# One long piece of projections per attention step, and value products between the two heads' transpositions

## The chip, the cores and the metric

The kernel runs on one NeuronCore of a Trainium2 chip. The metric is the device time of one execution in microseconds (us); the median of the runs shown is compared. TensorE is called PE here, VectorE DVE, ScalarE ACT, GpSimd POOL and the queue that issues most loads SP.

## The reference

A two-layer network over 256 latent and 256 context tokens (512 in all, width 1024). Each layer has four attention-like mixers that run side by side on one input projection, then an output projection, then a product-key expert network:

```python
(na_q, na_k, na_v, ml_qk, ml_v, ml_o, ml_g,
 mla_cq, mla_ckv, mla_kr, sw_q, sw_k, sw_v) = split_cols(h @ w_in)
...
y_a = neighbourhood_attention(...)      # 4 heads of 64
h_lat, h_ctx = mlstm_mixer(...)         # 4 heads
y_c = block_dense_attention(...)        # latent attention (MLA), keys from ckv and a shared rope part
y_d = window_attention(...)             # 4 query heads, 2 key heads, a sink
x = x + g1 * (jnp.concatenate([y_a, y_b, y_c, y_d], axis=-1) @ w_out)
...
f = peer_ffn(...)                       # top-16 of 128x128 experts for each of 8 heads
```

Layer 0 computes all 512 tokens in the mixers, layer 1 only the queries of the 256 latent ones. All data are 32-bit floats; projections are made of three products of a split operand (high and low parts).

## The kernel before

A layer is `mixers(l)` and then `peer(l)`. The expert part takes most of the time: layer 0's mixers run up to about 420 us of the span, its experts to about 1765 us, layer 1's mixers to about 1975 us, its experts to the end. The change lies in the mixers, in `run_units`.

**Units.** Each mixer makes units, one for each head and each block of 128 queries (`pairs`). A unit has 256 keys (query blocks 0 and 1, the context) or 512 keys (blocks 2 and 3). Units are worked off in pairs, the two heads of one query block. A mixer has 8 pairs in layer 0, two for each size twice over, and 4 pairs in layer 1, all of 512 keys. The order of the mixers is mLSTM (ML), neighbourhood (NA), latent attention (MLA), window (SW). For a pair PE makes the scores (`sc`), DVE and ACT make a softmax or the mLSTM's weights in SBUF (`soft`: for a softmax L582 the maximum, L588 the exponential with its sum, L592 and L593 the division), PE transposes each unit's weights into one PSUM bank (`tp`, L634; the pool `pst` has one buffer), ACT copies that to SBUF (L636), and PE multiplies by the values into `py` (L649). The scores of a pair are made one turn ahead, the value products one turn behind.

**The filler.** Projections that later mixers need are cut into small steps by generators. A `Filler` holds them in a queue, and `F.step(us)` issues steps until the sum of what they yield (an assumed time) reaches `us`, or until one yields 0:

```python
while us > 0:
    t = self._next()
    if t is None:
        return
    us -= t if t else us
```

So a step that yields 0 ends the whole call. The generators put such zeros where PE would wait for another engine: `mla_prep` (the normalisation, the rope and the small products of MLA) has 18 of them, two at the start and six before the scale of each of its two normalisations, one before each rope; `sw_prep` has one and `ada_end` four, at the end of layer 0's jobs for the modulation. Other steps are one k-block of a projection: three matmuls (L72, L73, L74), assumed at 0.65 us for 512 columns and 0.33 us for 256; for the modulation (L266, L267) two matmuls at 0.22 us. Before a mixer's first scores `F.finish(need)` issues without pause all that is left of the jobs which that mixer needs.

**A turn before.** The assumed time of one piece is `u.fill`: 1.3 us for ML in layer 0 and 2.0 in layer 1, 1.0 and 1.2 for NA, 1.2 and 1.2 for MLA, 1.2 and 1.0 for SW. A turn on a pair is: transpose the first unit; a piece; transpose the second unit; the next pair's scores; a piece; the last pair's value products; two pieces.

**What sets the order.** In the mixers PE's instructions stand as the program writes them (`manual_schedule`). The other engines, and PE in the expert part, are ordered by a scheduler that goes by its own estimate of times, so a change here can also move instructions elsewhere.

Of the kernel before, what the change touches and what calls it, by code (L numbers as in the profile page):

```python
# [8 lines left out]
F32 = mybir.dt.float32  # L9
# [44 lines left out]
class Kernel:  # L54
# [541 lines left out]
    def run_units(self, units):  # L596

        nc, F = self.nc, self.F  # L600
        n = len(units)
        p = {}
        py = None

        def score(i):
            if i >= n:
                return
            for u in units[i:i + 2 + AHEAD]:
                if u.pre:
                    F.finish(u.need)  # L610
                    u.pre()
                    u.pre = None
            both = units[i:i + 2]
            for u in both:
                F.finish(u.need)
            sc = [self.psc.tile([128, 512], F32, name="sc") for _ in both]
            steps = [u.score(x) for u, x in zip(both, sc)]
            while steps:
                steps = [g for g in steps if next(g, 0) is None]
            for j, u in enumerate(both):  # L620
                p[i + j] = u.soft(sc[j])
        score(0)
        F.step(1.0)
        F.step(1.0)
        last = None
        for i in range(0, n + 2, 2):
            both = units[i:i + 2]
            pts = []
            for j, u in enumerate(both):
                tp = self.pst.tile([128, 512], F32, name="tp")  # L630
                w = p.pop(i + j)
                nb = len(u.blocks)
                for x, kb in enumerate(u.blocks):
                    nc.tensor.transpose(tp[:, x * 128:(x + 1) * 128], w[:, kb * 128:(kb + 1) * 128], self.ident)  # L634
                pt = self.new()
                nc.scalar.copy(pt[:, :nb * 128], tp[:, :nb * 128])  # L636
                pts.append(pt)
                if j:
                    score(i + 2)
                F.step(u.fill)  # L640
            if last is not None:
                vs, vts = last
                if vs[0].first:
                    py = self.psy.tile([128, 512], F32, name="py")
                for x in range(max(len(v.blocks) for v in vs)):
                    for v, vt in zip(vs, vts):
                        nb = len(v.blocks)
                        if x < nb:
                            nc.tensor.matmul(py[v.rows, v.qt * 128:(v.qt + 1) * 128], v.v(v.blocks[x]), vt[:, x * 128:(x + 1) * 128],  # L649
                                             start=(x == 0), stop=(x == nb - 1))  # L650
                if vs[1].done:
                    vs[1].done(py)
                for v in vs:
                    F.step(v.fill)
            last = both, pts

    def put_y(self, ft, py, mul=None):
# [1145 lines left out]
```

## Time and profile before

| | us |
|---|---|
| median of the runs | 2815.85 |
| the profiled execution, its time | 2815.21 |
| its span | 2813.4 |
| PE busy in the span | 2649.8 |
| DVE busy | 2166.6 |
| ACT busy | 1244.3 |

The span is what the trace covers; its times count from the span's start. A wait that the timeline names in brackets is idle time of that engine just ahead of the row, with the instruction that ended it. Busy time of PE is modelled from starts and sizes, so the difference between two starts is the better price of a row. The granted clock is a mean over a stretch: 1.00 is 2.4 GHz all along, 0.50 would be 1.2 GHz all along.

### The profile page before, as it was taken

The page shows a single profiled execution, that of the slowest core. Times are in us where ns is not written, and L with a number is a line of the kernel's source. Part 1 is how long each engine was busy: PE and PEld are TensorE (multiplying, and loading weights), DVE is VectorE, ACT ScalarE, POOL GpSimd, SP SyncE. Part 2 cuts the span into 40 slices and gives each one's busy share as a digit, 9 for nine tenths or more (in the row PEclk, how much of TensorE's full clock was granted, in tenths as well). Part 3 has the DMA queues.
Part 4 walks back from the last instruction along what each step waited for, and adds up shares of the span by engine and source line. Part 5 has one row for each costly group of instructions (what it writes and reads, how often), then busy time and mean ns, then how long its engine had stood idle before and what let it go on. Part 6 is the DMA issues. An engine that isn't in the chain of part 4 may idle for free. (4 is left out here: it accounts for less than half of the span.)

```text
span 2813.4 us, 46689 instructions
## 1 busy us (share of the span) xinstructions
PE 2649.8 (94%) x18167; PEld 2446.7 (87%) x18167; DVE 2166.6 (77%) x4491; ACT 1244.3 (44%) x2059; POOL 478.8 (17%) x419
## 2 busy tenths in 40 slices
PE   8989899999999998899999998988999999899998
PEld 5766768999998898899999997767899999899998
DVE  5665657999998875799999887555888778577765
ACT  5564635334443443333333334644544445344443
POOL 0010000003333333234333310100001101211110
PEclk9999899999999999899999999999999999999999
DMA  7110424647999989899999993202545878888884
GB/s 266 65 61 31 165 90 161 225 148 262 351 371 332 339 325 377 306 361 382 384 374 376 376 322 115 77 33 72 203 145 188 299 266 306 319 310 304 292 292 161
DMA packets 275742, 691.62 MB, mean 246 GB/s; under 512 B 18016, under 2 KB 145376, under 8 KB 266048
## 3 DMA queue, kind: packets, MB, share of 16 engines
q1 hardware_dynamic: 196608, 448.12, 45.6%
q0 software_dynamic: 46080, 167.79, 15.8%
q10 hardware_dynamic: 32832, 72.72, 6.9%
q8 instruction: 142, 2.33, 0.3%
q14 instruction: 80, 0.66, 0.1%
HBM read 616.56 MB, written 71.57 MB: 245 GB/s over the span
## 5 line engine op out<-in xcount | busy, mean ns | idle before, releaser
L72 PE MATMUL pu<-h2h,spl 128*128 128x384 f32 (+1 forms) x2048 | 637.3, 311 | 40.7 <-ACT spl L1448 27.7
L73 PE MATMUL f<-wl,spl 128*128 128x384 f32 (+1 forms) x2048 | 623.9, 306 | 8.0 <-DVE wl L1502 8.0
L74 PE MATMUL pu<-h2h,spl 128*128 128x384 f32 (+1 forms) x2048 | 628.9, 308 | 2.6 <-DVE spl L1449 2.6
L73 PE MATMUL pu<-h2l,spl 128*128 128x384 f32 (+1 forms) x2048 | 629.5, 307 | 0.0
L74 PE MATMUL f<-wh,spl 128*128 128x384 f32 (+1 forms) x2048 | 609.7, 305 | 2.3 <-DVE spl L1506 2.3
L72 PE MATMUL f<-wh,spl 128*128 128x384 f32 (+1 forms) x2048 | 568.4, 307 | 8.8 <-ACT act L1466 4.6
L72 PEld LDWEIGHTS pu<-h2h,spl 128*128 128x128 f32 x2048 | 393.2, 192 | 49.6 <-ACT spl L1448 32.4
L73 PEld LDWEIGHTS f<-wl,spl 128*128 128x128 f32 x2048 | 391.5, 191 | 10.9 <-DVE wl L1502 10.4
L74 PEld LDWEIGHTS pu<-h2h,spl 128*128 128x128 f32 x2048 | 392.7, 192 | 4.4 <-DVE spl L1449 4.2
L72 PEld LDWEIGHTS f<-wh,spl 128*128 128x128 f32 x2048 | 386.0, 191 | 10.7 <-ACT act L1466 5.0
L73 PEld LDWEIGHTS pu<-h2l,spl 128*128 128x128 f32 x2048 | 393.3, 192 | 0.3
L1505 ACT CAST spl<-raw 128x1024 fp32r<-128x1024 f32 x256 | 264.9, 1050 | 289.5 <-DMA raw<-in_v 202.8
L74 PEld LDWEIGHTS f<-wh,spl 128*128 128x128 f32 x2048 | 385.8, 191 | 2.8 <-DVE spl L1506 2.8
L1506 DVE TENSOR_TENSOR spl<-raw,spl 128x1024 fp32r<-128x1024 f32 x256 | 308.4, 1219 | 93.4 <-ACT spl L1505 85.1
L1448 ACT CAST spl<-raw 128x1024 fp32r<-128x1024 f32 x256 | 265.7, 1048 | 240.3 <-DMA raw<-in_ut 94.8
L1449 DVE TENSOR_TENSOR spl<-raw,spl 128x1024 fp32r<-128x1024 f32 x256 | 310.3, 1218 | 47.9 <-ACT spl L1448 38.3
L1409 POOL DMA_INDIRECT spl<-in_un,ix x97 | 129.3, 1333 | 716.7 <-DVE fp L1263 241.6
L1466 ACT ACTIVATE act<-pu 128x384 f32<-128x384 f32 (+1 forms) x216 | 93.0, 435 | 303.8 <-PE pu L74 280.7
L427 DVE TENSOR_TENSOR spl<-raw,spl 128x512 fp32r<-128x512 f32 (+1 forms) x226 | 149.4, 699 | 65.4 <-ACT spl L423 56.3
L1409 POOL DMA_INDIRECT row<-in_vn,ix x87 | 125.4, 1441 | 374.6 <-DVE facc L1422 316.3
L1501 ACT CAST wh<-va 128x768 fp32r<-128x768 f32 (+1 forms) x108 | 78.3, 725 | 231.3 <-DVE va L1500 131.6
L72 PE MATMUL fp<-s,spl 128*128 128x512 f32 (+1 forms) x416 | 161.2, 387 | 2.1 <-DVE s L666 1.2
(319 smaller groups left out, 4459.0 us busy)
## 6 DMA issues: line engine op xcount, KB each, us to landing
raw<-in_ut SPq DMA_DIRECT2D x128, 1024.0 KB
raw<-in_v SPq DMA_DIRECT2D x128, 1024.0 KB
ad<-act ACTq DMA_DIRECT2D x64, 384.0 KB
gd<-gstage ACTq DMA_DIRECT2D x12, 2048.0 KB
vg<-gd SPq DMA_DIRECT2D x32, 768.0 KB
va<-ad SPq DMA_DIRECT2D x64, 384.0 KB
raw<-in_win SPq DMA_DIRECT2D x22, 1024.0 KB
raw<-in_wq SPq DMA_DIRECT2D x16, 1024.0 KB
```

What stands on the lines that cost most here:

```text
L72: mm(ps, ah, bh, start=first, stop=False, **kw)
L73: mm(ps, ah, bl, start=False, stop=False, **kw)
L74: mm(ps, al, bh, start=False, stop=last, **kw)
L427: return eng.tensor_tensor(p[1][o], w[:, o], p[0][o].bitcast(F32), op=ALU.subtract)
L1409: nc.gpsimd.indirect_dma_start(r, None, tabs[which], bass.IndirectOffsetOnAxis(ix[:, s:s + 1], 0))
L1448: self.pin(nc.scalar.copy(uh, self.u[:, n % 2]), n < 3)
L1449: self.pin(nc.vector.tensor_tensor(ul, self.u[:, n % 2], uh.bitcast(F32), op=ALU.subtract), n < 3)
L1466: nc.scalar.activation(a[:, b, :w], ps[:, :w], AF.Gelu)
L1501: nc.scalar.copy(wh, a[:, :, :w])
L1505: nc.scalar.copy(vh, v[:, b])
L1506: nc.vector.tensor_tensor(vl, v[:, b], vh.bitcast(F32), op=ALU.subtract)
```

## The change

A turn is now: transpose the first unit; the last pair's value products; transpose the second unit; the next pair's scores; then one call of `F.step` with four times `u.fill`.

```diff
--- before.py
+++ after.py
@@ -626,18 +626,19 @@
         for i in range(0, n + 2, 2):
             both = units[i:i + 2]
             pts = []
-            for j, u in enumerate(both):
-                tp = self.pst.tile([128, 512], F32, name="tp")
-                w = p.pop(i + j)
-                nb = len(u.blocks)
-                for x, kb in enumerate(u.blocks):
-                    nc.tensor.transpose(tp[:, x * 128:(x + 1) * 128], w[:, kb * 128:(kb + 1) * 128], self.ident)
-                pt = self.new()
-                nc.scalar.copy(pt[:, :nb * 128], tp[:, :nb * 128])
-                pts.append(pt)
-                if j:
-                    score(i + 2)
-                F.step(u.fill)
+
+            def turn(j):
+                if j < len(both):
+                    u = both[j]
+                    tp = self.pst.tile([128, 512], F32, name="tp")
+                    w = p.pop(i + j)
+                    nb = len(u.blocks)
+                    for x, kb in enumerate(u.blocks):
+                        nc.tensor.transpose(tp[:, x * 128:(x + 1) * 128], w[:, kb * 128:(kb + 1) * 128], self.ident)
+                    pt = self.new()
+                    nc.scalar.copy(pt[:, :nb * 128], tp[:, :nb * 128])
+                    pts.append(pt)
+            turn(0)
             if last is not None:
                 vs, vts = last
                 if vs[0].first:
@@ -650,8 +651,9 @@
                                              start=(x == 0), stop=(x == nb - 1))
                 if vs[1].done:
                     vs[1].done(py)
-                for v in vs:
-                    F.step(v.fill)
+            turn(1)
+            score(i + 2)
+            F.step(4 * (both or last[0])[0].fill)
             last = both, pts
 
     def put_y(self, ft, py, mul=None):
```

With the same numbers of instructions on PE, their order moves. Three places matter. The names: `tp` are transpositions, `py` value products, `sc` scores, `mm` products of `mla_prep` and the like, `fp` filler. Lines of the changed kernel after the edit are one to three higher.

First PE in layer 0's NA, a pair of 512 keys, from its scores to the next pair's. Before:

```order
L80 MATMUL sc<-s 128x512 x2
L82 MATMUL sc<-s 128x512 x2
L84 MATMUL sc<-s 128x512 x2
L719 MATMUL sc<-nab,con 128x256 x2
L649 MATMUL py<-s 64x128 x4
L634 MATMUL tp<-con,s 128x128 x4
L365 MATMUL mm<-s,ones 128x512
L634 MATMUL tp<-con,s 128x128 x4
L80 MATMUL sc<-s 128x512 x2
```

and changed:

```order
L80 MATMUL sc<-s 128x512 x2
L82 MATMUL sc<-s 128x512 x2
L84 MATMUL sc<-s 128x512 x2
L721 MATMUL sc<-nab,con 128x256 x2
L637 MATMUL tp<-con,s 128x128 x4
L650 MATMUL py<-s 64x128 x8
L637 MATMUL tp<-con,s 128x128 x4
L80 MATMUL sc<-s 128x256 x2
```

Before, the value products stood between the scores and the transpositions that wait for their softmax, and a product of `mla_prep` (L365) between the two transpositions. Now nothing stands between the scores and the first transposition, and the value products stand between the two. In layer 0's NA this holds for eight pairs in a row, apart from one product of `mla_prep` behind the scores of the first pair (L731) and of the third (L379), where before all the products of `mla_prep` and, from the seventh pair on, pieces of projections were spread over the eight.

Second PE at the start of layer 0's MLA, `mla_prep`. Before, its last steps stood among NA's units:

```order
L365 MATMUL mm<-s,ones 128x512
L807 MATMUL mm<-s,ukv 128x512
L649 MATMUL py<-s 64x128 x8
L807 MATMUL mm<-s,ukv 128x512
L815 MATMUL mm<-ukv,s 128x256 x4
L823 MATMUL mm<-s,uq 128x512 x2
L634 MATMUL tp<-con,s 128x128 x2
L823 MATMUL mm<-s,uq 128x512 x2
L634 MATMUL tp<-con,s 128x128 x2
```

and changed, all that was left by then is issued by `F.finish` behind NA's last transposition:

```order
L637 MATMUL tp<-con,s 128x128 x4
L365 MATMUL mm<-s,ones 128x512
L379 MATMUL mm<-s,ones 128x512 x2
L365 MATMUL mm<-s,ones 128x512
L809 MATMUL mm<-s,ukv 128x512 x2
L817 MATMUL mm<-ukv,s 128x256 x4
L825 MATMUL mm<-s,uq 128x512 x4
L731 MATMUL mm<-s,con 128x256
L825 MATMUL mm<-s,uq 128x512 x2
```

The second normalisation (L379 twice, then L365) is now two neighbouring rows; before, nine rows of NA's units (transpositions, scores and value products of two turns) stood between them.

Third PE in layer 0's SW, behind the last job of the modulation (L285). Before:

```order
L649 MATMUL py<-s 64x128 x4
L634 MATMUL tp<-con,s 128x128 x8
L80 MATMUL sc<-s 128x256 x2
L82 MATMUL sc<-s 128x256 x2
L84 MATMUL sc<-s 128x256 x2
L285 MATMUL mm<-cmb,adarow 128x2 x2
L649 MATMUL py<-s 64x128 x8
L634 MATMUL tp<-con,s 128x128 x4
L80 MATMUL sc<-s 128x256 x2
L82 MATMUL sc<-s 128x256 x2
L84 MATMUL sc<-s 128x256 x2
```

and changed:

```order
L768 MATMUL sc<-con 128x128 x2
L637 MATMUL tp<-con,s 128x128 x4
L650 MATMUL py<-s 64x128 x4
L637 MATMUL tp<-con,s 128x128 x4
L80 MATMUL sc<-s 128x512 x2
L82 MATMUL sc<-s 128x512 x2
L84 MATMUL sc<-s 128x512 x2
L770 MATMUL sc<-con 128x128 x2
L637 MATMUL tp<-con,s 128x128 x4
L650 MATMUL py<-s 64x128 x8
L637 MATMUL tp<-con,s 128x128 x4
```

Before, two pairs in a row had no filler, with value products behind each pair's scores; now three have none, with nothing behind their scores.

Where there is filler, a turn of ML in layer 0 has nine k-blocks in one piece behind the scores (four times 1.3 is eight steps of 0.65 and a rest of rounding, which takes a ninth), where it had two, the value products and four behind the scores and two between the transpositions. At the end of layer 0's mixers 24 k-blocks of the output projection stand behind the last value products up to the first of the sums of squares, before 8.

SP's list of loads is the same in the mixers; in layer 0's expert part the order of `raw`, `va`, `vg` and `adaw` loads against each other differs. POOL's list is the same throughout.

## Rows read from the trace of the kernel before

**Rows 1.** The page, part 1: busy time of each engine, share of the span, instructions.

```profile
PE 2649.8 (94%) x18167; PEld 2446.7 (87%) x18167; DVE 2166.6 (77%) x4491; ACT 1244.3 (44%) x2059; POOL 478.8 (17%) x419
```

**Rows 2.** Stretches: length, PE, PEld, DVE, ACT, POOL busy (count), clock, DMA, GB/s.

```profile
118.90:189.20 70.30, 65.13 (x323) 44.31 (x321) 41.29 (x177) 48.60 (x122) 13.82 (x29) 0.95 0.13 46
189.20:232.70 43.50, 35.94 (x205) 21.14 (x205) 27.29 (x81) 20.88 (x53) 2.07 (x2) 0.92 0.07 25
232.70:291.60 58.90, 55.43 (x333) 41.78 (x332) 34.40 (x83) 30.39 (x68) 0.00 (x0) 0.95 0.20 72
328.20:347.00 18.80, 14.69 (x87) 11.17 (x87) 10.56 (x37) 9.73 (x28) 0.00 (x0) 0.64 0.22 80
393.00:402.00 9.00, 6.01 (x55) 3.87 (x53) 5.16 (x14) 5.36 (x11) 0.00 (x0) 1.00 0.36 118
...
1790.30:1840.90 50.60, 47.03 (x262) 36.85 (x262) 30.18 (x107) 33.03 (x77) 5.96 (x13) 0.92 0.17 58
1840.90:1879.80 38.90, 31.04 (x186) 19.50 (x184) 23.32 (x66) 18.50 (x42) 1.72 (x2) 0.96 0.07 21
1910.60:1932.30 21.70, 14.58 (x97) 10.22 (x95) 12.78 (x35) 7.08 (x18) 0.00 (x0) 0.76 0.00 1
1932.30:1962.20 29.90, 28.57 (x258) 25.90 (x256) 18.89 (x52) 16.11 (x37) 0.00 (x0) 1.00 0.41 140
```

**Rows 3.** Timeline of PE, layer 0's ML: start, duration, instruction [idle before, ended by].

```profile
180.52 1.13 PE L966 MATMUL sc<-s 64*128 64x512 f32 x4
...
183.17 0.66 PE L649 MATMUL py<-s 128*64 128x128 f32 x8
...
184.56 0.40 PE L72 MATMUL fp<-s,spl 128*128 128x512 f32 x1
...
185.25 0.40 PE L72 MATMUL fp<-s,spl 128*128 128x512 f32 x1
...
186.82 0.63 PE L634 MATMUL tp<-con,s 128*128 128x128 f32 x4
```

**Rows 4.** Timeline of PE, layer 1's NA, a pair without projections.

```profile
1850.47 0.65 PE L634 MATMUL tp<-con,s 128*128 128x128 f32 x4 [0.68 <-ACT s L636]
1851.06 0.50 PE L80 MATMUL sc<-s 64*128 64x512 f32 x2
...
1853.01 1.09 PE L649 MATMUL py<-s 128*64 128x128 f32 x16
1855.45 0.63 PE L634 MATMUL tp<-con,s 128*128 128x128 f32 x4 [1.34 <-DVE st L592]
1855.91 1.02 PE L365 MATMUL mm<-s,ones 128*128 128x512 f32 x2
1856.77 0.63 PE L634 MATMUL tp<-con,s 128*128 128x128 f32 x4
1857.34 0.50 PE L80 MATMUL sc<-s 64*128 64x512 f32 x2
```

**Rows 5.** Timeline of PE, layer 0's NA: a pair of 256 keys.

```profile
218.73 0.41 PE L634 MATMUL tp<-con,s 128*128 128x128 f32 x2 [1.29 <-DVE st L592]
```

**Rows 6.** Timeline of PE, layer 1's SW: a softmax with a sink.

```profile
1923.13 1.59 PE L649 MATMUL py<-s 128*64 128x128 f32 x16
1926.34 0.63 PE L634 MATMUL tp<-con,s 128*128 128x128 f32 x4 [1.61 <-DVE st L591]
```

**Rows 7.** Timeline of PE: a normalisation's last product, of 512 and of 256 columns.

```profile
420.37 1.10 PE L365 MATMUL mm<-s,ones 128*128 128x512 f32 x2 [3.12 <-DVE s L360]
...
1973.21 0.70 PE L365 MATMUL mm<-s,ones 128*128 128x256 f32 x2 [1.90 <-DVE s L360]
```

**Rows 8.** Timeline of PE: the longest waits in ML, layer 0 and layer 1.

```profile
178.08 0.63 PE L634 MATMUL tp<-con,s 128*128 128x128 f32 x4 [2.73 <-DVE st L990]
...
1807.61 0.63 PE L634 MATMUL tp<-con,s 128*128 128x128 f32 x4 [2.97 <-DVE s L999]
```

**Rows 9.** Stretch of layer 0's experts, columns as in rows 2.

```profile
1100.00:1300.00 200.00, 181.10 (x1002) 179.06 (x1001) 156.19 (x190) 69.18 (x78) 60.36 (x45) 0.94 0.96 348
```

## The prediction

> **What bounds the kernel now.** The page's first part comes first: PE is busy in 94% of the span [rows 1]. So time is won or lost where PE waits, and otherwise only where its own work changes in length. The change leaves PE's work as it is and touches the mixers alone, so the second view is a table of PE's busy time by stretch [rows 2]: a stretch's length less PE's busy time is what PE waits there. In layer 0 that is 70.3 - 65.1 = 5.2 us in ML, 7.6 in NA with the end of `mla_prep`, 3.5 in the first part of MLA, 4.1 at the start of SW and 3.0 at SW's end; in layer 1 it is 3.6 in ML, 7.9 in NA, 7.1 at the end of MLA and the start of SW, and 1.3 after that. Together 43 us of some 280 + 172: all that a better order could give back, and the base on which a worse one adds.
>
> The third view is the timeline of PE, for three cases. With projections [rows 3], scores start at 180.52 and the first transposition at 186.82, without a wait: six k-blocks at 0.69 us (from 184.56 to 185.25) and the value products, 0.59 us, lie between. Without projections [rows 4], scores run from 1851.06 to 1853.01 and the transposition that needs their softmax starts at 1855.45, so the **softmax chain** takes 2.44 us from the end of the scores. Value products cover 1.1 us of it and PE waits 1.34. For a pair of 256 keys the same sum is 1.09 + 1.29 = 2.4 us [rows 5]; with a sink it is 1926.34 - 1923.13 = 3.2 us [rows 6]. Third, the second transposition waits 0.68 us for ACT to empty the one bank (the first row of [rows 4]).
>
> **The change, part by part.** The profiled execution took 2815.2 us, with a span of 2813.4; the median of the runs is 2815.85, so the sum is made against 2815.2. The order lists decide which pairs have filler behind their scores; those that have none I call bare.
>
> *Value products between the transpositions.* In a bare pair of 512 keys the turn before was 1.95 (scores) + 2.44 (chain, value products inside) + 0.46 + 0.68 + 0.17 + 0.57, some 6.3 us [rows 4]. Now it is 1.95 + 2.44 + 0.46, then value products of 0.6 to 1.0 in place of 0.68 + 0.17, then 0.57: 6.1 to 6.5. What is won behind the first transposition is lost ahead of it. I take 0 for this edit by itself; between the transpositions of pairs with filler it replaces two k-blocks, which had hidden the same copy.
>
> *One piece in place of four.* What costs is that a zero ends the whole turn's filler. `mla_prep` has 18 zeros. Four to a turn, they were used up in five turns; now each takes a turn, and NA in layer 0 has only eight. So all eight pairs of layer 0's NA are bare, the same holds for the four in layer 1, and the rest of `mla_prep` runs in one lump with nothing beside it.
>
> Layer 0's NA: 8 x 2.4 = 19.2, less what still stands behind two of the scores, 0.5 for half a product and 0.9 for a whole one (0.86 in rows 4), is 17.8 us. The lump has its second normalisation in neighbouring rows; such a wait took 3.1 us at 512 columns [rows 7], and I add two waits for emptied banks at 0.7 [rows 4]: 4.5. Together 22.3 in place of 7.6, so **+14.7**.
>
> Layer 0's MLA: the zero of `sw_prep` makes one bare pair, **+2.4**.
>
> Layer 0's SW: the four zeros at the end of the modulation make three bare pairs, where two were, and nothing covers their chain: 3 x 3.2 = 9.6 in place of 4.1, **+5.5**.
>
> Layer 0's end: more of the output projection is left over, and it now stands where PE waited for the last softmax and the last outputs. Of 3.0 I leave 0.7: **-2.3**.
>
> Layer 0's ML: between scores and first transposition there are now 9 x 0.69 = 6.2 us, before 4.1 + 0.6 to 1.0. The longest wait, 2.73 [rows 8], should shrink by about 1.3, the others by 0.4 in sum: **-1.7**.
>
> Layer 1's ML: the wait of 2.97 [rows 8] had four k-blocks ahead of it and now has sixteen; it goes. In the first turn no value products exist yet, so both transpositions stand together, and the second waits for its copy (0.68) and for its unit's weights, say 1.3: **-1.0**.
>
> Layer 1's NA: 4 x 2.4 - 0.5 - 0.9 = 8.2, and a lump of 1.9 [rows 7] + 1.4, in place of 7.9: **+3.6**.
>
> Layer 1, end of MLA and start of SW: one bare MLA pair more (+2.4), and the first SW pair pays 3.2 where it waited 1.6 [rows 6]; against that the second transpositions no longer wait alone, -2.3 from the 7.1 there: **+1.7**. After that the first output projection gets its last operand while transpositions and scores run: **-1.0**.
>
> The waits sum to +14.7 + 2.4 + 5.5 - 2.3 - 1.7 - 1.0 + 3.6 + 1.7 - 1.0 = **+21.9 us**.
>
> *The clock.* Where PE waits much, its granted clock falls [rows 2]: with 33% waits at SW's start in layer 1 it was 0.76, with 22% in layer 0's SW 0.64, while with 20% in layer 1's NA it stayed 0.96 and with 17% in layer 0's NA 0.92. The bare NA turns will wait about 40%: 2.4 of some 6.3 us with 512 keys, more with 256. PE's own work in a bare turn is 1.95 + 1.0 + 0.46 + 0.57 = 4.0 us with 512 keys [rows 4], and about half with 256: 24 us in layer 0's NA, 16 in layer 1's. At 0.76, the row nearest in waits, that work takes 1/0.76 - 1 = 32% longer; before it paid 9% and 4%. So 24 x 0.23 + 16 x 0.28 = **+10 us**. SW in layer 0 was at 0.64 and stays there: 0. The ends are 0 (the 0.96 row) and all of it at half speed, 24 x 0.91 + 16 x 0.96 + 10 x 0.44 = +42.
>
> The Trainium skill, page TensorE: Matmul & The Clock Gate, section "A second HAM failure mode: psum-queue depth-cycling", tells of a kernel in which short, frequent idle times of PE between groups of matmuls made the clock swing between its levels and cost throughput. By that rule these turns would come near the upper end; the trace has it both ways, 0.96 with 20% waits and 0.64 with 22%.
>
> *What moves elsewhere.* The scheduler puts SP's loads of layer 0's value stage in another order. PE waited 200 - 181.1 = 18.9 us in that stage's first 200 us [rows 9]. That whole amount is my bound to both sides; with no reason for a sign I take 0.
>
> Sum: 2815.2 + 21.9 + 10 = **2847 us**, 1.1% longer.
>
> **The rivals.** *The clock falls through.* If all bare turns run at the lower level, the clock costs 42 in place of 10: 2815.2 + 22 + 42 = 2879. [...] For it: 0.64 with 22% waits. Against it: 0.96 with 20%, and the lumps are dense work. 0.10.
>
> *The longer cover wins, and it is not slower.* If the zeros did not add bare pairs, the gains stay alone: -2.3 - 1.7 - 3.0 - 1.0, and nothing for the moved value products: -8, 2807. This decides if the chain, without evacuations and splits of weights on DVE and ACT between, shrinks so far that a bare turn waits no more than it did. Layer 0's NA would have to wait 3.1 us in eight turns, 0.4 each, beside the lump. For it: DVE was busy for 27.3 of 43.5 us in that stretch [rows 2], partly with other work. Against it: the 2.44 in rows 4 is little else than one unit's own steps. 0.15.
>
> *The piece is as long as its name.* That the change does not do what it says is part of the forecast: the piece is cut to nothing by each zero. If the turns of NA were filled in spite of it, the time would be the one just given.
>
> *The loads.* With the reordered loads worth their bound, the forecast becomes 2828 or 2866.
>
> **How the numbers follow.** The forecast has 0.75, fall of the clock 0.10, longer cover 0.15. The time is the forecast's, 2847. Its own range comes from 7 us of error on the waits (17 bare pairs at 0.4), the clock's lower end and part of the loads' bound: 2824 to 2870. The range for 8 in 10 goes a little into both rivals: 2815 to 2874. The bounds of 2%, about what a measurement of this kernel can tell from no change, are 2759 and 2871.5. Faster than that needs more than the 43 us of all waits: 0.02. Slower needs the fallen clock, or the forecast with loads and waits at their upper ends: 0.11. Within: 0.87.
>
> **What would show it.** In the profile after, the stretch of layer 0's NA should have PE waits near 22 us in place of 7.6, with waits of 2 to 2.5 us ahead of each first transposition, ended by DVE's division, and hardly one ahead of a second. A wait of about 3 us should stand ahead of the second L365 of the lump. Layer 0's SW should show three waits near 3 us; the long waits in ML of both layers should be gone or half. The clock in the NA stretches should be 0.7 to 0.8. The prediction is wrong if the waits ahead of first transpositions are well under 2 us, if the clock in those stretches stays above 0.9 (then near 2837), or if the experts' stretches change in length by more than a few us.

## The result, and the profile after

The changed kernel takes 2853.16 us (median of four runs, 2847.28 to 2858.59) where the kernel before takes 2813.07 beside it (median of four): a ratio of 1.014, with a 95% interval of 1.0109 to 1.0171. One of the four runs of the kernel before, of 3308.41 us, was a slow one and is left out of the ratio. So it is slower by 1.4%, inside the 2% that count as no change. The forecast was 2847 us, 1.1% longer. The profiled execution of the changed kernel took 2847.28 us, the least of its four.

The page of the changed kernel, part 1 (busy time, share of the span, instructions), beside [rows 1]:

```profile
span 2845.5 us, 46699 instructions
PE 2656.4 (93%) x18167; PEld 2454.5 (86%) x18167; DVE 2168.2 (76%) x4491; ACT 1242.3 (44%) x2059; POOL 488.9 (17%) x419
```

The number of instructions of PE is the same and its busy time has grown by 6.6 us; the span has grown by 32.1. The rest, 25.5, is waits. Where they are, the table of stretches shows; the columns are those of [rows 2]: bounds, length, busy time of PE, PEld, DVE, ACT and POOL (count), clock, DMA share, GB/s.

```profile
119.90:192.30 72.40, 68.23 (x354) 49.46 (x353) 43.85 (x181) 51.51 (x126) 13.54 (x29) 0.95 0.16 59
192.30:260.10 67.80, 48.12 (x252) 27.46 (x251) 32.84 (x94) 26.06 (x63) 2.03 (x2) 0.87 0.00 1
260.10:314.40 54.30, 46.37 (x314) 35.04 (x313) 29.41 (x79) 25.10 (x61) 0.00 (x0) 1.00 0.16 55
357.70:385.60 27.90, 15.63 (x93) 11.01 (x92) 12.45 (x37) 11.75 (x31) 0.00 (x0) 0.65 0.15 54
411.00:419.50 8.50, 8.44 (x63) 6.60 (x61) 2.87 (x6) 1.94 (x4) 0.00 (x0) 1.00 0.62 232
1816.00:1865.20 49.20, 47.40 (x286) 37.46 (x285) 31.23 (x109) 35.19 (x81) 5.98 (x13) 0.96 0.21 71
1865.20:1908.40 43.20, 31.85 (x181) 20.92 (x179) 22.20 (x63) 16.82 (x39) 1.90 (x2) 0.92 0.01 6
1938.00:1963.00 25.00, 14.65 (x82) 9.81 (x82) 12.25 (x34) 7.39 (x18) 0.00 (x0) 0.74 0.00 1
1963.00:1993.00 30.00, 29.86 (x266) 26.76 (x265) 19.76 (x51) 16.57 (x37) 0.00 (x0) 0.99 0.38 136
```

In their order: ML, NA with the rest of `mla_prep`, the first part of MLA, the start of SW and SW's end in layer 0; ML, NA, the end of MLA with SW's start, and what follows in layer 1. Length less PE's busy time gives the waits: 4.2, 19.7, 7.9, 12.3 and 0.1 us in layer 0 (1.8 more lie between the third and the fourth), 1.8, 11.4, 10.3 and 0.1 in layer 1. Together some 70 where 43 were. From the first scores of ML to the normalisation behind SW (the L365 of [rows 7]), layer 0's mixers are 28.1 us longer and layer 1's 5.3; the experts of layer 0 became 3.3 shorter, the end 1.2 longer.

The timeline of PE in layer 0's NA shows the new turn (start, duration, instruction, in brackets idle time before and what ended it; L637 is the transposition, L650 the value products):

```profile
210.25 0.51 PE L80 MATMUL sc<-s 64*128 64x512 f32 x2
...
211.15 1.13 PE L721 MATMUL sc<-nab,con 128*128 128x256 f32 x4
214.25 0.63 PE L637 MATMUL tp<-con,s 128*128 128x128 f32 x4 [1.98 <-DVE st L592]
214.81 1.09 PE L650 MATMUL py<-s 128*64 128x128 f32 x16
215.84 0.66 PE L637 MATMUL tp<-con,s 128*128 128x128 f32 x4
216.42 0.38 PE L80 MATMUL sc<-s 64*128 64x256 f32 x2
...
218.83 0.41 PE L637 MATMUL tp<-con,s 128*128 128x128 f32 x2 [1.78 <-DVE st L592]
```

Behind the scores stands nothing: PE waits for the division of the softmax, and not ahead of the second transposition, where the value products now cover ACT's copy. Eight such waits, of 1.12 to 2.29 us, sum to 14.4; seven end with the division, one with the exponential. The lump follows:

```profile
238.95 1.02 PE L365 MATMUL mm<-s,ones 128*128 128x512 f32 x2
240.32 1.98 PE L379 MATMUL mm<-s,ones 128*128 128x512 f32 x4 [0.34 <-ACT s L373]
245.32 1.13 PE L365 MATMUL mm<-s,ones 128*128 128x512 f32 x2 [3.02 <-DVE s L360]
251.50 1.13 PE L817 MATMUL mm<-ukv,s 128*128 128x256 f32 x4 [0.54 <-DVE s L91]
257.46 1.98 PE L825 MATMUL mm<-s,uq 128*128 128x512 f32 x4 [0.97 <-DVE s L91]
```

The second L365 waits 3.02 us, as its like did in [rows 7]; with the small ones the lump waits 4.9. At the start of layer 0's SW the timeline has these three, all on PE:

```profile
365.64 1.09 PE L637 MATMUL tp<-con,s 128*128 128x128 f32 x4 [6.31 <-DVE st L591]
374.00 1.09 PE L637 MATMUL tp<-con,s 128*128 128x128 f32 x4 [3.34 <-DVE st L591]
381.60 0.66 PE L637 MATMUL tp<-con,s 128*128 128x128 f32 x2 [2.62 <-DVE st L591]
```

### The profile page after: what moved, and what is told of

Same layout as the page of the kernel before. It is cut to its first block, busy times and chain, and to the rows that moved or that the text cites. A ratio compares the mean times of both kernels' runs of the same rounds, so it can differ in the third digit from the quotient of the medians.

```text
span 2845.5 us, 46699 instructions
## 1 busy us (share of the span) xinstructions
PE 2656.4 (93%) x18167; PEld 2454.5 (86%) x18167; DVE 2168.2 (76%) x4491; ACT 1242.3 (44%) x2059; POOL 488.9 (17%) x419
## 5 line engine op out<-in xcount | busy, mean ns | idle before, releaser
L72 PE MATMUL pu<-h2h,spl 128*128 128x384 f32 (+1 forms) x2048 | 636.2, 311 | 36.0 <-ACT spl L1450 26.6
L72 PEld LDWEIGHTS pu<-h2h,spl 128*128 128x128 f32 x2048 | 392.1, 191 | 44.5 <-ACT spl L1450 31.7
L72 PEld LDWEIGHTS f<-wh,spl 128*128 128x128 f32 x2048 | 386.5, 191 | 11.1 <-ACT spl L1507 4.0
L1451 DVE TENSOR_TENSOR spl<-raw,spl 128x1024 fp32r<-128x1024 f32 x256 | 312.2, 1227 | 40.0 <-ACT spl L1450 34.6
L1411 POOL DMA_INDIRECT spl<-in_un,ix x97 | 135.3, 1395 | 703.8 <-DVE fp L1265 241.6
L1502 DVE TENSOR_TENSOR va<-va,vg 128x768 f32<-128x768 f32 (+1 forms) x108 | 88.4, 821 | 95.8 <-DMA va<-ad 77.7
```

The source lines that it names most:

```text
L72: mm(ps, ah, bh, start=first, stop=False, **kw)
L1411: nc.gpsimd.indirect_dma_start(r, None, tabs[which], bass.IndirectOffsetOnAxis(ix[:, s:s + 1], 0))
L1451: self.pin(nc.vector.tensor_tensor(ul, self.u[:, n % 2], uh.bitcast(F32), op=ALU.subtract), n < 3)
L1502: nc.vector.tensor_mul(av, av, self.vg[:, :w // 32, i % 4:i % 4 + 2].rearrange("p q b t -> p b q t"))
```

## The experiments

**The theory** is the one of the prediction: with one long piece each zero of a generator makes a turn bare, a bare turn costs its softmax chain, and the clock adds to that; where the value products stand is worth nothing in a bare turn. **The rivals:** the new place of the value products costs by itself; or it is the clock alone; or something outside the mixers. The last one the profile settles: the rest of the span changed by +0.8 us ahead of ML, -3.3 in layer 0's experts and +1.2 at the end.

The kernel before takes other times on other chips (2802.74, 2804.12 and 2811.53 us, medians of 15, 20 and 27 runs, beside the three groups of experiments), so ratios are compared. In the second group the changed kernel itself ran again, with 1.0143 (1.0114 to 1.0173).

> The changed kernel itself, beside the others on this chip. Both theories expect the ratio of 1.014 again, about 2842 us where the kernel before takes 2803.

The lengths and waits in this table are of one profiled execution each, on different chips: from ML's first scores to the normalisation behind SW in layer 0, and in that stretch the length less PE's busy time, summed over the four mixers. The change itself took 327.6 and 330.2 us there in its two profiled executions, so a difference of 2 to 3 us between two rows says nothing.

| kernel | ratio (95% interval) | layer 0's mixers, us | waits there, us |
|---|---|---|---|
| before | 1 | 299.5 | 26.6 |
| the change | 1.0140 (1.0109 to 1.0171) | 327.6 | 49.1 |
| four calls | 1.0006 (0.9994 to 1.0019) | 302.9 | 31.7 |
| value products behind the scores | 1.0230 (1.0201 to 1.0259) | 341.9 | 54.4 |
| bare turns filled with idle products | 1.0122 (1.0090 to 1.0155) | 322.0 | 29.3 |
| no zeros at the modulation's end | 1.0096 (1.0066 to 1.0126) | 312.2 | 38.6 |
| 6 zeros of 18 in `mla_prep` | 1.0023 (1.0003 to 1.0042) | 304.5 | 32.7 |
| both of these | 1.0011 (0.9992 to 1.0031) | 299.1 | 30.8 |
| four calls, 10 zeros, none at the end | 1.0086 (1.0060 to 1.0112) | 320.5 | 40.0 |
| 6 zeros, none at the end, shorter pieces | 0.9979 (0.9962 to 0.9997) | 296.7 | 27.4 |
| zeros filled, shorter pieces | 0.9989 (0.9972 to 1.0006) | 301.9 | 29.1 |
| turn of before, 10 zeros, shorter pieces | 0.9990 (0.9972 to 1.0008) | 298.0 | 26.3 |

**Four calls in place of the long one**, all else as in the change:

```diff
-            F.step(4 * (both or last[0])[0].fill)
+            for _ in range(4):
+                F.step((both or last[0])[0].fill)
```

> The changed turn, but with four calls of one fill in place of one call of four fills, so that a zero ends a quarter only; the value products stay between the transpositions. My theory (the zeros make the bare turns): NA, MLA and SW of layer 0 go back to about the waits of before (7.6, 3.5 and 4.1 us), the gains in ML and at the ends stay, so about 5 us under the kernel before: 2800 to 2818 us. Rival (the value products' new place costs the time): it stays above 2835 us.

Measured 1.0006: the whole cost of the change goes when a zero may end only a quarter of a turn's filler. The value products are still between the transpositions, so their place is not the cost. (Four calls also round otherwise than one, in layer 0 by at most one k-block a turn.) The expected gain over the kernel before did not come: ML's waits in layer 0 fell to 2.2, but 10.5 stood in MLA and 9.8 in SW, where 7.1 and 6.8 had been.

**The value products behind the scores again**, with the long piece kept:

```diff
             turn(0)
+            turn(1)
+            score(i + 2)
             if last is not None:
...
-            turn(1)
-            score(i + 2)
             F.step(4 * (both or last[0])[0].fill)
```

> The changed kernel with its one long piece, but the value products back behind the scores. My theory: a bare turn is as long either way, since what the value products cover of the softmax they no longer cover of the copy; so layer 0's NA and the lump keep their 67.8 us within 3, and the turns with filler pay the copy between the transpositions, 0.4 to 0.7 us in some 25 turns: 2856 to 2870 us. Rival (uncovered softmax, because the value products left): layer 0's NA falls under 60 us and the whole under 2845 us.

Measured 2863.39 us, 1.023: by the ratios some 25 us above the change, where 3 to 17 were expected. A bare pair of 512 keys in layer 0's NA of this kernel, PE's timeline (L652 is the value products here):

```profile
210.61 0.50 PE L80 MATMUL sc<-s 64*128 64x512 f32 x2
...
212.57 0.66 PE L652 MATMUL py<-s 128*64 128x128 f32 x8
214.67 0.63 PE L637 MATMUL tp<-con,s 128*128 128x128 f32 x4 [1.45 <-DVE st L592]
215.97 0.80 PE L637 MATMUL tp<-con,s 128*128 128x128 f32 x4 [0.68 <-ACT s L639]
216.71 0.58 PE L80 MATMUL sc<-s 64*128 64x256 f32 x2
```

From scores to scores it takes 216.71 - 210.61 = 6.10 us; the same pair of the change, with twice as many value products, took 216.42 - 210.25 = 6.17. One wait of 1.98 has become 1.45 + 0.68. So in a bare turn the place is worth nothing, as predicted; NA is 66.3 us long against 67.8. What this kernel adds to the change comes from turns with filler, where nothing now stands between the two transpositions: layer 0's MLA is 13.0 us longer, its ML 2.8, layer 1's mixers 6.7. Of MLA's 13.0 only 5.5 are waits; the rest is PE's work, at a clock of 0.87 where the change had 0.96, and that the expectation had left out.

**Bare turns filled with idle products.** Where the call issued no filler, eight matmuls of 512 columns are added whose result nobody reads (the diff leaves out that `F.step` now returns the sum of what it issued):

```diff
-            F.step(4 * (both or last[0])[0].fill)
+            if not F.step(4 * (both or last[0])[0].fill) and i + 2 < n:
+                ps = self.psf.tile([128, 512], F32, name="fp")
+                for k in range(KD):
+                    nc.tensor.matmul(ps, self.hh[k][:, 0:128], self.hh[k], start=(k == 0), stop=(k == KD - 1))
```

> The changed kernel with eight matmuls of 512 columns, which nothing reads, behind the scores of each turn that got no filler (ten in layer 0, four in layer 1): some 1.9 us of PE work in waits of 2 to 3 us. If the clock is part of the cost, it goes to 0.95 or more in both NA stretches and the time falls by 5 to 10 us against the changed kernel, to 2840 to 2849 us. If the waits for DVE and ACT alone set it, it stays within 3 us of the changed kernel.

Measured 1.0122. The stretches of layer 0's NA, of its SW and of layer 1's NA in this kernel:

```profile
191.46:255.43 63.97, 53.71 (x298) 33.71 (x297) 32.19 (x94) 25.87 (x63) 2.21 (x2) 0.97 0.00 1
337.57:442.55 104.98, 96.38 (x551) 73.89 (x551) 61.53 (x173) 46.25 (x113) 1.01 (x1) 0.95 0.31 111
1851.68:1893.43 41.75, 33.95 (x195) 22.40 (x195) 22.21 (x63) 16.84 (x39) 1.90 (x2) 0.96 0.01 4
```

Layer 0's NA has 48 more matmuls than the change and is 3.8 us shorter, with its clock at 0.97 in place of 0.87 (in the change's second profiled execution NA took 69.9 us at 0.82). Layer 0's mixers are 5.6 us shorter, layer 1's 4.9: in these two executions about the 10 us of the forecast. For the whole kernel that is not shown: its ratio is 0.0018 below the change's, some 5 us, inside both intervals, and the profiled execution took 2821.57 us where the median is 2831.58. The waits themselves were only filled, not won. The Trainium skill, page TensorE: Matmul & The Clock Gate, section "A second HAM failure mode: psum-queue depth-cycling", puts such a loss to short, frequent idle times between groups of matmuls; the trace agrees, with 0.87 where PE paused in all eight turns of layer 0's NA and 0.97 where it paused in two of them.

**No zeros at the modulation's end**, in the changed kernel:

```diff
     def ada_end(self):
-        for _ in range(4):
-            yield 0
+        yield 0.1
         self.ada_turn()
```

> The changed kernel without the four zeros at the end of layer 0's modulation. My theory: the three bare turns at SW's start get filler, their waits (12.3 us in the profile, in 27.9 us at a clock of 0.65) go down to 2 or less, and the time falls by 10 to 16 us: 2837 to 2844 us. Rival (the filler used there is only missing later, at the end): within 4 us of the changed kernel.

Measured 1.0096. The stretch of SW in layer 0:

```profile
340.30:433.24 92.94, 86.32 (x528) 66.54 (x527) 60.45 (x170) 45.80 (x111) 1.01 (x1) 1.00 0.36 125
```

It was 109.53 with 92.85 busy and a clock of 0.89, over as many matmuls: 16.6 us shorter, 10.1 of it waits and 6.5 the clock. NA is as it was. So four steps without any work cost 17 us in this stretch; by the ratio the whole gained 0.0044, some 12 us, as expected.

**6 of the 18 zeros of `mla_prep`** (two fall to one, six to one), and **the same without the end's zeros**:

```diff
         yield 0
-        yield 0
         ps = self.bank()
...
-        for _ in range(6):
+        for _ in range(1):
             yield 0
```

> The changed kernel with its long piece; of the 18 zeros of mla_prep 6 are left (two fall to one, six to one). Theory (the price is one bare turn for each zero): in layer 0 the projections of mla_prep spread over the neighbourhood mixer, three to five of its eight pairs are bare and there is no lump, so that stretch falls from 67.8 to 57 to 60 us, in layer 1 from 43 to 39 to 41. What was issued there is missing later: SW in layer 0 gets one more bare pair, 3 us. Whole: 6 to 12 us below the changed kernel, 2830 to 2836. Rival (the length of the piece or the place of the value products costs by itself): within 3 us of the changed kernel.

> As the one with 6 zeros, and the four zeros at the end of the modulation are one step of cost 0.1. Theory: the two gains add (6 to 12 from the neighbourhood mixer, 18 as measured without the end's zeros), less 6 for two bare pairs at the start of SW, since the filler now runs out there: 2812 to 2822, still above the kernel before. Rival (all of the change's price is zeros, and the long piece and the moved value products gain what is left): 2795 to 2803.

Measured 1.0023 and 1.0011. Layer 0's NA, first in the change (as it ran in this group), then with 6 zeros, then without the end's zeros too:

```profile
191.62:261.51 69.89, 49.88 (x251) 28.89 (x250) 32.63 (x94) 25.92 (x63) 2.03 (x2) 0.82 0.00 1
```

```profile
191.00:249.04 58.04, 50.33 (x277) 31.86 (x276) 32.04 (x95) 25.77 (x63) 2.03 (x2) 0.91 0.00 1
```

```profile
191.78:248.92 57.14, 48.75 (x277) 30.78 (x276) 31.85 (x95) 25.66 (x63) 2.03 (x2) 0.94 0.00 1
```

Layer 0's NA came out as expected (58.0 for 57 to 60), layer 1's is 36.5 us where 39 to 41 were expected. The whole did not: the first was expected 6 to 12 us below the change and is 0.012 of the ratio below it, some 34 us. What was left out of that expectation is in the columns: 26 more matmuls (work that layer 0 would have had to do later) now run inside the shorter NA, and MLA and SW together are 13.8 us shorter, 4.7 of it waits, the rest work already done and a higher clock. The one more bare pair that was expected in SW did not come. PE's timeline of this kernel has three there, as the change has:

```profile
336.72 0.66 PE L636 MATMUL tp<-con,s 128*128 128x128 f32 x2 [5.34 <-DVE st L590]
343.59 0.41 PE L636 MATMUL tp<-con,s 128*128 128x128 f32 x2 [2.75 <-DVE st L590]
351.08 0.89 PE L636 MATMUL tp<-con,s 128*128 128x128 f32 x4 [3.13 <-DVE st L590]
```

In MLA it has none, where the change had one (2.18). The filler was not missing later, since the change had left 24 k-blocks of the output projection over behind its last value products and this kernel leaves 8. The second kernel shows the bound: the two savings, 0.0120 and 0.0044 of the ratio, do not add (together 0.0132); that both draw on the same filler is a reading, not shown. With 2806.72 us it lies between its two expected ranges (2795 to 2803 and 2812 to 2822).

**Four calls, 10 of the 18 zeros, none at the end** (two fall to one and six to three, in two normalisations, beside the two of the ropes: that leaves 10, where the expectations of this kernel and of the last one say 9):

> Four short pieces again, the value products between the transpositions as in the change, half of the zeros of mla_prep (9 of 18), one step of 0.1 at the end of the modulation. Theory: with four pieces a turn the zeros were absorbed anyway, and fewer of them only move bare turns from the neighbourhood mixer to the end of MLA and the start of SW, where the filler runs out before the output projection's jobs exist: 2798 to 2810, the same as the kernel before. Rival (zeros cost in any length of piece): 2790 to 2797, faster than the kernel before.

Measured 1.0086, outside both expectations. Two rows of PE's timeline in layer 0, the first in `mla_prep`, the second in SW:

```profile
212.71 2.08 PE L364 MATMUL mm<-s,ones 128*128 128x512 f32 x2 [4.62 <-DVE s L359]
...
341.86 1.09 PE L635 MATMUL tp<-con,s 128*128 128x128 f32 x4 [3.06 <-DVE st L590]
```

With four calls a turn and few zeros `mla_prep` is issued so fast that PE waits inside it for the normalisation, and the filler is used up by the end of MLA: four transpositions there and at SW's start wait 2.6 to 3.1 us each, and MLA's clock is 0.81. So zeros are not a cost as such. With short calls they stretched the filler to where it is needed; too few of them cost as well.

**Shorter pieces.** If a bare turn is the price and 2.4 or 3.2 us of cover are enough, the 8 k-blocks of a turn are more than it needs. So `u.fill` is cut, in the kernel with 6 zeros and none at the end:

```diff
-F_ML, F_NA, F_MLA, F_SW = (1.3, 2.0), (1.0, 1.2), (1.2, 1.2), (1.2, 1.0)
+F_ML, F_NA, F_MLA, F_SW = (1.1, 1.6), (0.8, 0.65), (0.65, 0.65), (0.95, 0.95)
```

> The long piece with 6 zeros in mla_prep, none at the end of the modulation, and shorter pieces: u.fill of 1.1 and 1.6 (ML), 0.8 and 0.65 (NA), 0.65 and 0.65 (MLA), 0.95 and 0.95 (SW), so 5 or 6 k-blocks a turn where 8 were, 3.4 to 4.1 us. By the order no pair of SW is bare then, in either layer; three or four of NA still are. Theory (a bare turn is the price, and 2.4 or 3.2 us of cover are enough): the waits of layer 0's SW fall from 11.1 us (e7) to 4 to 6, layer 1's end of MLA and SW from 13.3 to 8, the clock there rises to 0.96: 2790 to 2800, ratio 0.995 to 0.999. Rival (DVE and ACT do the filler's own work between, so the chain with filler is longer than 3.4 us and each turn waits 0.5 more, 24 turns): 2808 to 2818.

Measured 0.9979, inside the 0.995 to 0.999 expected: the one kernel of eleven whose interval lies below 1, and its upper end is 0.9997. SW in layer 0, which begins earlier here and takes over more of the filler:

```profile
303.55:416.81 113.26, 104.41 (x657) 83.89 (x657) 75.78 (x200) 60.26 (x142) 1.01 (x1) 0.98 0.44 155
```

Its waits are 8.9 us (4 to 6 were expected, 11.1 with the long pieces); the last normalisation's 3.1 is in them, which no filler reaches. No transposition of it waits 2 us any more, and the clock is 0.98. In layer 1 the end of MLA and SW wait 10.4 us, not the 8 expected: `sw_prep` ahead of SW's scores still costs its 2.8, and the first SW pair there is bare after all (3.14).

The next kernel replaces zeros of `mla_prep` by k-blocks of the projection of SW's queries. That has 16 k-blocks, so two of the 18 zeros stay. The diff leaves out the lines that join the two jobs, the four zeros at the modulation's end, which are gone here too, and the pieces, which are those above but 0.8 for NA in layer 1 and for MLA in layer 0:

```diff
+    def mixed(self, a, b):
+        for t in a:
+            yield t or next(b, 0)
+        yield from b
```

> The long piece, all 18 zeros of mla_prep kept, but each zero is replaced by one k-block of the projection of SW's queries, so that it doesn't end the piece; no zeros at the end of the modulation; shorter pieces (0.8, 0.65 and 0.95). By the order no pair of layer 0's NA is bare, and at most two pairs in each layer at all. Theory (the zeros cost only because they make turns bare): NA's waits in layer 0 fall from 8 to 10 to 2 to 4, in layer 1 from 8 to 3 to 5, and SW's as with the shorter pieces: 2778 to 2792, ratio 0.991 to 0.996. Rival (single k-blocks at the zeros don't cover the other engines' work, so PE waits inside mla_prep instead): 2795 to 2806.

Measured 0.9989, on the rival's side. Layer 0's NA and MLA:

```profile
186.56:247.14 60.58, 57.08 (x328) 38.74 (x327) 36.89 (x102) 32.06 (x75) 2.21 (x2) 1.00 0.10 35
247.14:326.01 78.87, 65.96 (x421) 51.67 (x421) 44.92 (x117) 38.42 (x92) 0.00 (x0) 0.83 0.24 89
```

NA waits 3.5 us, as the theory said, and its clock is 1.00. In layer 1 NA waits 7.4, where 3 to 5 were expected. Layer 0's MLA waits 12.9, most of it in five waits: 3.06 in a bare pair, 2.19 inside `sw_prep`, 1.98 in a small step of the modulation, and 2.27 and 2.17 ahead of second transpositions, for ACT's copy. The rival's place was wrong (inside `mla_prep` PE waits only 1.4 us), its number right. Last, the turn of the kernel before with the shorter pieces and 10 zeros:

> The turn of the kernel before (four short pieces, the value products behind the scores), with 9 of the 18 zeros of mla_prep, none at the end of the modulation and the shorter pieces. It asks whether the turn's form matters once few turns are bare. Theory (the form is worth little, bare turns are all): 2790 to 2802, within 8 us of the long piece with shorter pieces. Rival (with 1 k-block and the value products behind the scores and 2 more behind those, the short form covers less of the chain): 2806 to 2820.

Measured 0.9990, 6.8 us above the long piece with shorter pieces in the medians, where up to 8 were expected. With few bare turns the two forms of the turn are alike in layer 0: 298.0 and 296.7 us, 26.3 and 27.4 of waits. In layer 1 the mixers take 185.2 and 180.9. The two kernels also differ in their zeros, 10 against 6, so the form of the turn is not tested by itself.

## Why the prediction was right, step by step

The mechanism was the one predicted, and the kernels with four calls and with fewer zeros show it by removal: without the zeros' power over a whole turn the cost is gone. Its terms:

*Layer 0's NA and the lump*: 22.3 us of waits forecast, 19.7 measured. The lump was right (4.5 and 4.9), the bare turns overpriced (17.8 and 14.4). The chain in [rows 4] held other work: in that pair DVE also emptied a finished pair of value products between the steps of the softmax. Three rows of the kernel before show it (start, duration; PE, then DVE):

```profile
1851.95 1.13 PE L719 MATMUL sc<-nab,con 128*128 128x256 f32 x4
...
1854.15 0.42 DVE L663 TENSOR_TENSOR s<-py,s 128x256 f32<-128x256 f32 x1 [0.18 <-PE py L649]
...
1854.61 0.29 DVE L666 CAST s<-s 128x256 fp32r<-128x256 f32 x1
```

From the mask's product (1851.95 there, 211.15 in the change) to the transposition it took 3.50 us, now 3.10. *Layer 1's NA*: 11.5 forecast, 11.4 measured.

*Layer 0's SW*: 9.6 forecast, 12.3 measured. Three bare pairs, as said, and two at 3.34 and 2.62 as priced; the first waited 6.31. The rows behind it, of DVE and ACT in the change:

```profile
358.54 2.00 DVE L427 TENSOR_TENSOR spl<-raw,spl 128x512 fp32r<-128x512 f32 x3 [1.73 <-ACT spl L423]
360.91 0.69 DVE L427 TENSOR_TENSOR spl<-raw,spl 128x512 fp32r<-128x512 f32 x1 [0.37 <-ACT spl L423]
361.52 0.68 DVE L582 TENSOR_REDUCE st<-sc 128x1 f32<-128x512 f32 x1
362.12 0.68 DVE L427 TENSOR_TENSOR spl<-raw,spl 128x512 fp32r<-128x512 f32 x1
362.72 0.68 DVE L582 TENSOR_REDUCE st<-sc 128x1 f32<-128x512 f32 x1
...
360.26 1.14 ACT L423 CAST spl<-raw 128x512 fp32r<-128x512 f32 x2 [0.45 <-DMA raw<-in_wout]
```

Splits of the output projection's weight stand on DVE ahead of the softmax's maxima and between them, and wait there for ACT's halves, which waited 0.45 us for the weight's load. The forecast counted bare turns on PE and did not ask what else DVE had in its queue there.

*Layer 0's MLA*: 5.9 forecast, 7.9 measured; besides the bare pair (2.18) `sw_prep` waits 1.79 inside itself. *Layer 1's end of MLA and SW's start*: 8.8 and 10.3. There `sw_prep` now stands directly ahead of SW's first scores, and these wait 2.86 us for its last split on ACT; the forecast had priced the pairs and not that:

```profile
1952.79 0.50 PE L80 MATMUL sc<-s 64*128 64x512 f32 x2 [2.86 <-ACT s L90]
```

*ML and the ends*: 3.5 forecast and 4.2 measured in layer 0, 2.6 and 1.8 in layer 1; the ends 0.7 and 0.3 forecast, 0.1 measured in each. One long wait is left in layer 0's ML, of 3.03 us; the others are gone.

*The waits in sum*: +21.9 forecast, +27 measured over the eight mixers.

*The clock*: +10 forecast. With each mixer's busy time of PE times one less its clock, before and after, the eight stretches give +8.4; PE's busy time over the same matmuls grew by 6.1 in them. Its places were wrong: the bare turns of layer 0's and layer 1's NA ran at 0.84 and 0.88, not 0.76:

```profile
195.30:239.00 43.70, 30.74 (x205) 20.01 (x206) 22.01 (x63) 18.43 (x48) 1.02 (x1) 0.84 0.00 1
1870.00:1898.70 28.70, 20.70 (x134) 14.04 (x134) 14.38 (x46) 11.13 (x25) 1.90 (x2) 0.88 0.00 1
```

And layer 0's SW, taken at nothing since it was at 0.64 already, stayed there for 27.9 us in place of 18.8 and cost +6. Of the signs that the prediction named, two came out short: the whole NA stretches had 0.87 and 0.92, not 0.7 to 0.8, and the second is above the 0.9 that it called a sign of being wrong; and the waits ahead of layer 0's first transpositions were 1.8 us in the mean, not 2 to 2.5.

*Loads*: 0 forecast. Experts and end together changed by -2.1.

So the sum, 2847 against 2847.3 of the profiled execution and 2853.2 of the median, was right in its mechanism, with errors of 2 to 3 us in most terms. That it hits the profiled execution to 0.3 us is luck: the waits came out 5 us higher, the clock and the rest of the span 5 lower, and that execution lies 6 us below the median. The ratio of 1.014 puts the growth at 39 us, where 32 were forecast. Of the rivals, the fallen clock (2879) and the longer cover (2807) did not come (the second takes layer 1's ML at a gain of 3.0, where the sum has 1.0; with 1.0 it is 2809); the value products' place was rightly taken at 0 in bare turns.

What is still open: why MLA's clock fell to 0.83 with 16% waits in the kernel with the filled zeros, while the change's first part of MLA kept 1.00 with 15%. And the gain of the shorter pieces, 0.2%, is of the size of its own interval.

## What to carry to other kernels

A piece of cover is as long as what ends it, not as long as its name: before pieces that cover a latency are merged, count the steps that end one early and the turns these leave bare. Cover that is longer than the chain it hides is taken from a later turn; cut it to the chain, and the filler lasts (worth 0.2% here, hardly more than its interval). A chain priced from one row contains what else the other engine did in that row, and leaves out what it will have to do at the new place.

## What the runs showed of the hardware

Idle products paid in their stretch: with 48 more matmuls layer 0's NA was 3.8 us shorter, at a clock of 0.97 in place of 0.87. For the whole kernel the gain lies inside the intervals. And a microsecond of waits cost more than itself here: in layer 0's mixers the change took 10.5 us more waits than the kernel without the end's zeros and was 15.4 us longer, and 21.7 more than the one with shorter pieces and 30.9 longer, about 1.4 to 1.5 us for one; what is over is PE's work at a lower clock, over as many matmuls. The share of waits alone does not tell the clock: it was 0.65 with 44%, 0.87 with 29%, 0.83 with 16% and 0.64 with 22% [rows 2].
